# A later weight tile's parts moved behind the second norm's diagonals, and side work held one step earlier

## The chip, the cores and the metric

The kernel runs on one core of a Trainium2 chip. The metric is the device time of one execution in microseconds (us); the median of three runs of the kernel before is 1535.8 us (1535.44 to 1537.49).

## What is computed

One layer of a hybrid decoder block in float32, on 256 rows of width 2048. Cut to what matters here:

```python
mod = SiLU(c) @ ada_w + ada_b            # shift1, scale1, gate1, shift2, scale2, gate2
h   = RMSNorm(x) * (1 + scale1) + shift1
merged = sigmoid(g_A) * (lru(h) @ w_lru_out) + sigmoid(g_B) * (attention(h) @ w_attn_out)
x   = x + gate1 * (merged @ w_o)
h2  = RMSNorm(x) * (1 + scale2) + shift2                     # the second norm
x   = x + gate2 * ((silu(gate) * up) @ w_ffn_out)            # gate, up = h2 @ w_ffn_in
out = RMSNorm(x)
```

## The kernel before

All weights are read once from HBM, in tiles of 128 x 1024 floats (512 KB) that are called items here and numbered in the order of use. Each matmul is done in three products of rounded floats: a weight tile `raw` is split into `hi` (a rounding cast, on ScalarE, `do_hi`, L330) and `lo` (raw minus hi, on VectorE, `do_lo`, L342), an activation likewise, and `mm3` (L380 to L384) multiplies high by high, high by low and low by high. A full item takes 12 matmuls of 512 columns.

The order on every engine is written out by the program. `step(i)` (L349) issues, for item i: the loads up to item i + AHEAD (6) on SyncE's DMA queue, the high parts up to i + N_HI (4) on ScalarE, the low parts up to i + N_LO (3) on VectorE, then the item's matmuls on TensorE, then side work. `raw` has five buffers, `hi` four, `lo` three. Each engine takes its instructions strictly in that order.

Side work here is `ada`: for each of the 96 tiles of 128 values of `mod` (but one) two multiply-and-sum instructions over a 128 x 1024 tile `aw` (L532, VectorE), each with a 512 KB load of its own. `run_sides` places them by a rough clock that the program keeps, wherever that says VectorE has room (`clock["slack"]`); what is not placed in one step comes in a later one. The last of them must be done before the gate of the feed-forward's output is needed.

Around the change stand the last steps of `w_o` (items 268 to 275, the last of its four slabs) and the second norm. `hold_sides` (L1087), put before the last but one step of `w_o`, sets the slack so low that no side work is placed from there on. In the last step the products are sorted so that the first 128 rows' bank is complete half a step before the second's. `second_norm` (L1111) then runs ahead of the next item's step: four transposes for each of x's first four pairs of tiles (`turn`, L1100), and for each half of the rows y = bank * gate1 (L1120), x += y (L1121) and the sum of squares (L1122, ScalarE); two more turns; the root (L1130), its reciprocal, two diagonal blocks, one on VectorE (L1135), one on ScalarE (L1136); two warming matmuls, the product of ones by the diagonals (`r2_ps`, L1139), which lays 1/rms out along the rows, and five more warming matmuls (a float32 matmul shows as two instructions). From `r2_ps` come the normed tiles: `scaled` (L1148, VectorE), `high` (L1156, ScalarE), `low` (L1161, VectorE), pair by pair. Items 276 on are the feed-forward's first weights (`fg`), whose first matmul needs the high part of the first normed tile and whose third needs its low part.

After two slabs of that kind (items 276 to 291) come pairs of slabs in which some blocks are done by seven products for eight; there VectorE also makes sums of weights (`wy`, L458, L459), and `lo` is cut from those sums too.

Of the kernel before, what the change touches and what calls it, by code (L numbers as in the profile page):

```python
# [42 lines left out]
AHEAD, N_HI, N_LO, N_ADA, N_B4 = 6, 4, 3, 2, 25  # L43
# [40 lines left out]
def hybrid_layer(  # L84
# [33 lines left out]
    def wtile(name):  # L118
        return ps.tile([P, 2, S], F32, tag="bank", name=name)
# [8 lines left out]
    def rows(t):  # L128
        return slice(t * P, (t + 1) * P)
# [28 lines left out]
    def keep_warm(n, of_w=False):  # L158

        warm = in_rows_of(wtile("warm")) if of_w else mtile("warm")  # L160
        for _ in range(n):
            nc.tensor.matmul(warm[:, 0:P], lhsT=ones, rhs=ones, start=True, stop=True)
        free(m=0 if of_w else 1)
# [60 lines left out]
    def charge(dve=0.0, act=0.0):  # L224
        clock["dve"] = max(clock["dve"], clock["pe"]) + dve
        clock["act"] = max(clock["act"], clock["pe"]) + act
# [10 lines left out]
    def run_posts():  # L237
        for g in list(posts):
            try:
                charge(*next(g))  # L240
            except StopIteration:
                posts.remove(g)
# [29 lines left out]
    def run_sides(end):  # L272
        for s in sides:
            for _ in range(s.most):
                if s.cost is None:
                    break
                if max(clock["dve"], clock["pe"]) + s.cost[0] > end + clock["slack"]:
                    if s.fits():
                        return
                    break  # L280
                if max(clock["act"], clock["pe"]) + s.cost[1] > end + clock["slack"] or not s.advance():
                    break


    class Item:


        def __init__(self, src, cols, mm, post=None, keep=False, weight=1, used=None, before=()):
# [3 lines left out]

            self.sums = None

    items = []
    live = {}
    at = {"fill": 0, "add": 0, "load": 0, "made": 0, "hi": 0, "lo": 0}

    def do_sum(j):
        def do(i):  # L300
            if items[i].sums is not None:
                items[i].sums[j]()
                load_time(CH)
        return do
# [42 lines left out]
    def upto(what, fn, n):  # L347
        while at[what] < min(n, len(items)):
            fn(at[what])  # L349
            at[what] += 1  # L350

    def step(i):
        it = items[i]
        if not items[min(i + N_LO, len(items)) - 1].keep:
            run_posts()
        upto("load", do_load, i + AHEAD)
        upto("made", do_made, i + N_MADE)
        upto("hi", do_hi, i + N_HI)
        upto("lo", do_lo, i + N_LO)
        if items[min(i + N_LO, len(items)) - 1].keep:  # L360
            run_posts()
        upto("fill", do_sum(0), i + N_SUM[0])
        upto("add", do_sum(1), i + N_SUM[1])
        for stage in it.before:
            charge(*stage())
        for h in streams:
            h.fetch()
        _, hi, lo, t = live.pop(i)
        clock["pe"] = max(clock["pe"], t)
        end = clock["pe"] + it.cols * T_PE * it.weight  # L370
        it.mm(hi, lo)
        run_sides(end)
        clock["pe"] = end
        if it.post is not None:
            posts.append(it.post())
# [686 lines left out]
    def o_post(s):  # L1062
        def post(banks):
            if s == 3:
                second_norm(banks)
                return
            if s == 2:
                early_root()
            y = b4(f"yo{s}", F32, (2, 512))
            for t in range(2):  # L1070
                nc.vector.tensor_tensor(y[:, t, :], in_rows_of(banks[t]), g1_of(s), op=ALU.mult)
            yield 1.4, 0
            nc.vector.tensor_tensor(xr[s], xr[s], y, op=ALU.add)
            yield 1.13, 0
            for t in range(2):
                nc.scalar.activation(y[:, t, :], xr[s][:, t, :], AF.Square, accum_out=ss2[:, t, s:s + 1])
            keep_rows(s)
            free(b4=1)
            yield 0, 1.6
        return post  # L1080
# [8 lines left out]
        clock["slack"] = -1e9  # L1089
        return 0, 0  # L1090

    items[-2].before.append(hold_sides)

    def turn(p, of_w=False):

# [15 lines left out]
    def second_norm(banks):  # L1111
# [22 lines left out]
        r2, diag = b4("r2")[:, 0, :], y[:, 0, 0:S]  # L1134
        nc.vector.tensor_scalar(diag[:, rows(0)], ident, sr[:, 0:1], None, op0=ALU.mult)  # L1135
        nc.scalar.activation(diag[:, rows(1)], ident, AF.Copy, scale=sr[:, 1:2])  # L1136
        r2_ps = wtile("r2_ps")[:, 0, :]
        keep_warm(N_WARM_2[0], True)
        nc.tensor.matmul(r2_ps, lhsT=ones, rhs=diag, start=True, stop=True)  # L1139
# [540 lines left out]
    for i in range(len(items)):  # L1680
        step(i)
# [63 lines left out]
```

## Time and profile before

| | |
|---|---|
| median of three runs | 1535.8 us (1535.44 to 1537.49) |
| the profiled execution | 1538.73 us, its span 1537.0 us |
| granted TensorE clock over the span | 0.998 of full speed |
| TensorE matmuls busy | 1521.0 us, 99% of the span |
| VectorE busy | 1365.3 us, 89% |
| ScalarE busy | 880.7 us, 57% |
| GpSimd busy | 163.5 us, 11% |
| the chain that ended last, by engine | TensorE 93%, DMA 3%, VectorE 3% |

Busy time is the time in which an engine runs instructions, loads of weights into TensorE apart. In the profile PE is TensorE, DVE VectorE, ACT ScalarE, SP SyncE and POOL GpSimd. [...]

### The profile page before, as it was taken

How to read it: one execution, taken by the hardware profiler on the slowest of the kernel's cores; microseconds unless marked ns; L12 is line 12 of the kernel's file. 1: busy time of each engine (PE TensorE's matmuls, PEld its weight loads, DVE VectorE, ACT ScalarE, POOL GpSimd, SP SyncE). 2: the span in 40 equal slices, each digit the busy share in tenths (PEclk: the TensorE clock that was granted, in tenths of full speed). 3: DMA queues.
4: the chain of work that ended last, by engine and by line, in shares of the span. 5: the costliest groups of instructions: out<-in, count | busy, mean ns of one | idle time of the engine just before them, and what ended most of it. 6: DMA issues, size and time to landing. Idle time of an engine off the chain costs nothing.

```text
span 1537.0 us, 20204 instructions
## 1 busy us (share of the span) xinstructions
PE 1521.0 (99%) x6851; PEld 1249.0 (81%) x6851; DVE 1365.3 (89%) x1835; ACT 880.7 (57%) x1142; POOL 163.5 (11%) x232
## 2 busy tenths in 40 slices
PE   8999999999999999999999999999999999999997
PEld 5788888888888787888887878888888888888886
DVE  7999999888898888988988899999999999888987
ACT  4654444886964446444444556656665556664664
POOL 0000000000000000000002231034212122321200
PEclk9999999999999999999999999999999999999999
DMA  9999988656786887999999999589898979989983
GB/s 368 383 345 362 345 315 301 207 181 217 241 286 226 291 308 283 364 325 341 377 373 347 312 338 273 167 254 332 274 273 248 269 243 298 288 257 297 275 266 124
DMA packets 138440, 444.58 MB, mean 289 GB/s; under 512 B 16064, under 2 KB 16224, under 8 KB 138336
## 3 DMA queue, kind: packets, MB, share of 16 engines
q1 hardware_dynamic: 113056, 384.02, 70.2%
q0 software_dynamic: 24992, 58.75, 16.1%
q8 instruction: 53, 0.87, 0.2%
q10 hardware_dynamic: 288, 0.52, 0.1%
q14 instruction: 51, 0.42, 0.1%
HBM read 439.02 MB, written 4.21 MB: 288 GB/s over the span
## 4 chain that ended last, share of the span: by engine, by line
PE 93%; DMA 3%; DVE 3%; ACT 0%; issue 0%; SPq 0%; DVEq 0%; ACTq 0%
PE pf L1391 10%; PE f L383 6%; PE f L382 6%; PE f L384 6%; PE wi L383 6%; PE wi L384 6%; PE wi L382 6%; PE wl L384 2%; PE wl L383 2%; PE wga L384 2%; PE wl L382 2%; PE wga L382 2%; PE wgl L383 2%; PE wga L383 2%; PE wgl L384 2%; PE wa L384 2%
## 5 line engine op out<-in xcount | busy, mean ns | idle before, releaser
L330 ACT CAST hi<-raw 128x1024 fp32r<-128x1024 f32 (+1 forms) x540 | 532.3, 996 | 419.1 <-PE wi L384 87.4
L342 DVE TENSOR_TENSOR lo<-raw,hi 128x1024 fp32r<-128x1024 f32 (+1 forms) x540 | 611.9, 1149 | 82.1 <-issue 37.7
L383 PE MATMUL wi<-lo,h 128*128 128x512 f32 x432 | 168.4, 390 | 3.3 <-DVE lo L342 3.3
L382 PE MATMUL wi<-hi,h 128*128 128x512 f32 x432 | 169.9, 393 | 0.0
L384 PE MATMUL wi<-hi,h 128*128 128x512 f32 x432 | 168.2, 389 | 0.0
L382 PE MATMUL f<-hi,h 128*128 128x512 f32 x406 | 158.8, 391 | 0.0
L383 PE MATMUL f<-lo,h 128*128 128x512 f32 x406 | 158.1, 389 | 0.0
L384 PE MATMUL f<-hi,h 128*128 128x512 f32 x406 | 158.0, 389 | 0.0
L532 DVE CUSTOM_DVE_ANT_0 aw<-aw,crow,vec 128x1024 f32<-128x1024 f32 x95 | 120.5, 1277 | 6.0 <-DMA aw<-in_ada_t_dram 6.0
L532 DVE CUSTOM_DVE_ANT_0 aw<-aw,crow,modc 128x1024 f32<-128x1024 f32 x95 | 121.1, 1277 | 1.6 <-DMA aw<-in_ada_t_dram 1.6
L330 ACT CAST hi<-wy 128x1024 fp32r<-128x1024 f32 x55 | 58.0, 1055 | 74.3 <-PE f L384 32.1
L383 PEld LDWEIGHTS wi<-lo,h 128*128 128x128 f32 x432 | 81.1, 188 | 20.9 <-DVE lo L342 4.3
L342 DVE TENSOR_TENSOR lo<-wx,hi 128x1024 fp32r<-128x1024 f32 x55 | 67.2, 1222 | 32.4 <-issue 28.5
L330 ACT CAST hi<-wx 128x1024 fp32r<-128x1024 f32 x55 | 58.0, 1055 | 64.8 <-PE pf L1391 24.0
L382 PEld LDWEIGHTS wi<-hi,h 128*128 128x128 f32 x432 | 81.1, 188 | 16.8 <-ACT acc L611 0.2
L384 PEld LDWEIGHTS wi<-hi,h 128*128 128x128 f32 x432 | 81.1, 188 | 16.7
L384 PEld LDWEIGHTS f<-hi,h 128*128 128x128 f32 x406 | 76.2, 188 | 15.8
L383 PEld LDWEIGHTS f<-lo,h 128*128 128x128 f32 x406 | 76.2, 188 | 15.7 <-DVE lo L342 0.3
L382 PEld LDWEIGHTS f<-hi,h 128*128 128x128 f32 x406 | 76.2, 188 | 15.6
L447 POOL DMA_DIRECT2D wx<-in_w_f_dram x78 | 69.8, 969 | 79.5 <-DMA wx<-in_w_f_dram 78.4
L443 POOL DMA_DIRECT2D wx<-in_w_f_dram x78 | 44.7, 627 | 287.6 <-DVE lo L342 95.2
L342 DVE TENSOR_TENSOR lo<-wy,hi 128x1024 fp32r<-128x1024 f32 x55 | 67.2, 1222 | 6.9 <-ACT hi L330 4.3
(347 smaller groups left out, 3094.1 us busy)
## 6 DMA issues: line engine op xcount, KB each, us to landing
aw<-in_ada_t_dram SPq DMA_DIRECT2D x190, 512.0 KB, 6.7
raw<-in_w_in_dram SPq DMA_DIRECT2D x164, 512.0 KB, 5.1
raw<-in_w_f_dram SPq DMA_DIRECT2D x137, 512.0 KB, 6.5
wx<-in_w_f_dram POOLq DMA_DIRECT2D x156, 256.0 KB, 7.9
raw<-in_w_f2a_dram SPq DMA_DIRECT2D x36, 512.0 KB, 6.4
raw<-in_w_lru_dram SPq DMA_DIRECT2D x32, 512.0 KB, 4.6
raw<-in_w_att_dram SPq DMA_DIRECT2D x32, 512.0 KB, 5.5
raw<-in_w_o_dram SPq DMA_DIRECT2D x32, 512.0 KB, 8.1
```

What stands on the lines that cost most here:

```text
L330: nc.scalar.copy(hi[:, cs], live[i][0][:, cs])
L342: nc.vector.tensor_tensor(lo[:, cs], raw[:, cs], f32(hi[:, cs]), op=ALU.subtract)
L382: nc.tensor.matmul(ps, lhsT=lh, rhs=rh, start=start, stop=False, skip_group_check=True)
L383: nc.tensor.matmul(ps, lhsT=lh, rhs=rl, start=False, stop=False, skip_group_check=True)
L384: nc.tensor.matmul(ps, lhsT=ll, rhs=rh, start=False, stop=stop, skip_group_check=True)
L443: nc.gpsimd.dma_start(x[:, j * 512:(j + 1) * 512], block(0, 1))
L447: nc.gpsimd.dma_start(got["x"][:, j * 512:(j + 1) * 512], block(j, j), accum_op=ALU.add)
L532: nc.vector.tensor_tensor_reduce(out=r, in0=r, in1=crow[j], op0=ALU.mult, op1=ALU.add, scale=1.0, scalar=dst if j else vec[:, v:v + 1], ac ...
L1391: nc.tensor.matmul(bank(t, n), lhsT=l[:, rows(t)], rhs=w[:, c0:c0 + 512], start=kt == 0 and k == 0, stop=kt == (EARLY - 2 if (t, n) == (1, ...
```

## The change

Side work is held from the last step but two of `w_o` on, not the last but one. In the last step of `w_o` the high and the low parts go one item less far ahead (`parts_wait`), and the two parts that are left out there, the high part of item 278 and the low part of item 277, are issued inside `second_norm` right behind the two diagonal blocks. Nothing is added or removed.

```diff
@@ -292,6 +292,8 @@
             self.sums = None
+            self.parts_wait = 0
...
@@ -355,8 +357,9 @@
         upto("load", do_load, i + AHEAD)
         upto("made", do_made, i + N_MADE)
-        upto("hi", do_hi, i + N_HI)
-        upto("lo", do_lo, i + N_LO)
+
+        upto("hi", do_hi, i + N_HI - it.parts_wait)
+        upto("lo", do_lo, i + N_LO - it.parts_wait)
...
@@ -1089,7 +1092,8 @@
         clock["slack"] = -1e9
         return 0, 0
-    items[-2].before.append(hold_sides)
+    items[-3].before.append(hold_sides)
+    items[-1].parts_wait = 1
...
@@ -1134,6 +1138,9 @@
         nc.vector.tensor_scalar(diag[:, rows(0)], ident, sr[:, 0:1], None, op0=ALU.mult)
         nc.scalar.activation(diag[:, rows(1)], ident, AF.Copy, scale=sr[:, 1:2])
+
+        upto("hi", do_hi, at["hi"] + 1)
+        upto("lo", do_lo, at["lo"] + 1)
         r2_ps = wtile("r2_ps")[:, 0, :]
```

TensorE's and GpSimd's order is the same in both. The lines of the changed kernel are higher by 2 to 7 (L342 is L344 there, L532 is L535, L1120 is L1124, L1148 is L1155).

VectorE from the last two steps of `w_o` to the first normed tile (`lo275` is the last item of `w_o`, `aw` with its line L532 is side work, shown as two instructions). Before:

```order
L342 TENSOR_TENSOR lo275_6925<-raw275_6858,hi275_6902 128x1024
L532 ISA aw179_6886,modc_162<-aw179_6886,crow0_108,vec_74 128x1024
L532 ISA modc_162 128x1
L342 TENSOR_TENSOR lo276_6946<-raw276_6880,hi276_6923 128x1024
L342 TENSOR_TENSOR lo277_6964<-raw277_6900,hi277_6944 128x1024
L1120 TENSOR_TENSOR yo3_7008<-wo3_0_0_6821,g11_6095 128x512
L1121 TENSOR_TENSOR xr3_6819<-xr3_6819,yo3_7008 128x512
L1120 TENSOR_TENSOR yo3_7008<-wo3_0_1_6822,g11_6095 128x512
L1121 TENSOR_TENSOR xr3_6819<-xr3_6819,yo3_7008 128x512
L1106 COPY x1T1_7024<-pt1_6993 128x512
L1129 TENSOR_REDUCE sr_7023<-ss2_176 128x2
```

And now, up to the first normed tile:

```order
L344 TENSOR_TENSOR lo275_6925<-raw275_6858,hi275_6902 128x1024
L344 TENSOR_TENSOR lo276_6945<-raw276_6880,hi276_6923 128x1024
L1124 TENSOR_TENSOR yo3_7003<-wo3_0_0_6821,g11_6095 128x512
L1125 TENSOR_TENSOR xr3_6819<-xr3_6819,yo3_7003 128x512
L1124 TENSOR_TENSOR yo3_7003<-wo3_0_1_6822,g11_6095 128x512
L1125 TENSOR_TENSOR xr3_6819<-xr3_6819,yo3_7003 128x512
L1110 COPY x1T1_7019<-pt1_6988 128x512
L1133 TENSOR_REDUCE sr_7018<-ss2_176 128x2
L1135 RECIPROCAL sr_7018<-sr_7018 128x2
L1139 TENSOR_SCALAR yo3_7003<-ident_92,sr_7018 128x128
L344 TENSOR_TENSOR lo277_7039<-raw277_6900,hi277_6943 128x1024
L1155 SCALAR_TENSOR_TENSOR x1T0_7007<-x1T0_7007,modc_162,r2_ps_7041 128x256 x2
```

Two instructions are gone from in front of the norm's first one, the multiply `aw179` and `lo277`; `lo277` now stands between the diagonal block and the first `scaled`.

ScalarE at the same place, now (before, the cast `hi278` stood right behind `hi277`):

```order
L332 CAST hi277_6943<-raw277_6900 128x1024
L1126 ACTIVATE yo3_7003,ss2_176<-xr3_6819 128x512
L1110 COPY x1T0_7007<-pt0_6983 128x512
L1126 ACTIVATE yo3_7003,ss2_176<-xr3_6819 128x512
L1134 ACTIVATE sr_7018<-sr_7018,eps_t_90 128x2
L1140 ACTIVATE yo3_7003<-ident_92,sr_7018 128x128
L332 CAST hi278_7037<-raw278_6921 128x1024
L1163 ACTIVATE h2_0_6975<-x1T0_7007,modc_162 128x256 x2
```

The cast moved from ahead of the squares to ahead of the first `high`.

The multiply that is not done before the norm pushes the ones behind it on. Eleven now stand behind the norm where ten stood. The last of them are in the first pair of slabs on VectorE. Before:

```order
L342 TENSOR_TENSOR lo304_7664<-raw304_7625,hi304_7651 128x1024
L532 ISA aw189_7558,modc_162<-aw189_7558,crow1_109,modc_162 128x1024
L532 ISA modc_162 128x1
L458 TENSOR_TENSOR wy_7681<-wx_7432,raw305_7635 128x512
L459 TENSOR_TENSOR wy_7681<-wy_7681,raw304_7625 128x512
L342 TENSOR_TENSOR lo305_7686<-raw305_7635,hi305_7662 128x512
L342 TENSOR_TENSOR lo306_7704<-wx_7432,hi306_7684 128x1024
```

Now:

```order
L344 TENSOR_TENSOR lo304_7663<-raw304_7624,hi304_7650 128x1024
L535 ISA aw188_7530,modc_162<-aw188_7530,crow1_109,modc_162 128x1024
L535 ISA modc_162 128x1
L461 TENSOR_TENSOR wy_7680<-wx_7430,raw305_7634 128x512
L462 TENSOR_TENSOR wy_7680<-wy_7680,raw304_7624 128x512
L344 TENSOR_TENSOR lo305_7685<-raw305_7634,hi305_7661 128x512
L535 ISA aw189_7602,modc_162<-aw189_7602,crow1_109,modc_162 128x1024
L535 ISA modc_162 128x1
L344 TENSOR_TENSOR lo306_7704<-wx_7430,hi306_7683 128x1024
```

Between `lo304` and `lo306` there are two multiplies where there was one. On SyncE's queue three of the loads of `aw` (185, 187 and 189) have moved behind one weight load each.

## Rows read from the trace of the kernel before

**Rows 1.** The page: busy time of TensorE (share of the span, instructions), and the chain that ended last, by engine.

```profile
PE 1521.0 (99%) x6851; PEld 1249.0 (81%) x6851; DVE 1365.3 (89%) x1835; ACT 880.7 (57%) x1142; POOL 163.5 (11%) x232
PE 93%; DMA 3%; DVE 3%; ACT 0%; issue 0%; SPq 0%; DVEq 0%; ACTq 0%
```

**Rows 2.** What TensorE waited for over the whole span: engine, tile and line that waited, who ended the wait, us in total, times, longest.

```profile
PE pt L1100 <- DVE xr L1121: 1.0, 1, 1.0
PE r_ps L1139 <- ACT yo L1136: 0.9, 1, 0.9
```

**Rows 3.** Timeline of VectorE around the second norm and, last, in the slab behind it: start us, us, engine, line, operation, out<-in, shapes, count, and in brackets the idle time before and what ended it.

```profile
820.63 1.28 DVE L532 CUSTOM_DVE_ANT_0 aw<-aw,crow,vec 128x1024 f32<-128x1024 f32 x1 [2.02 <-DMA aw<-in_ada_t_dram]
821.84 1.22 DVE L342 TENSOR_TENSOR lo<-raw,hi 128x1024 fp32r<-128x1024 f32 x1
823.40 1.23 DVE L342 TENSOR_TENSOR lo<-raw,hi 128x1024 fp32r<-128x1024 f32 x1 [0.34 <-ACT hi L330]
824.54 0.68 DVE L1120 TENSOR_TENSOR yo<-wo,g 128x512 f32<-128x512 f32 x1
...
825.87 0.68 DVE L1120 TENSOR_TENSOR yo<-wo,g 128x512 f32<-128x512 f32 x1
...
828.80 0.29 DVE L1135 TENSOR_SCALAR yo<-ident,sr 128x128 f32<-128x128 f32 x1
830.12 0.87 DVE L1148 SCALAR_TENSOR_TENSOR x1T<-x1T,modc,r_ps 128x256 f32<-128x256 f32 x2 [1.03 <-PE r_ps L1139]
831.23 0.89 DVE L1161 SCALAR_TENSOR_TENSOR h<-x1T,modc,h 128x256 fp32r<-128x256 f32 x2 [0.24 <-ACT h L1156]
...
834.68 1.21 DVE L342 TENSOR_TENSOR lo<-raw,hi 128x1024 fp32r<-128x1024 f32 x1
...
854.82 1.23 DVE L342 TENSOR_TENSOR lo<-raw,hi 128x1024 fp32r<-128x1024 f32 x1 [1.50 <-PE fg L383]
```

**Rows 4.** Timeline of ScalarE there, same columns.

```profile
822.32 1.05 ACT L330 CAST hi<-raw 128x1024 fp32r<-128x1024 f32 x1 [3.54 <-DMA raw<-in_w_f_dram]
824.88 1.05 ACT L330 CAST hi<-raw 128x1024 fp32r<-128x1024 f32 x1 [1.51 <-DMA raw<-in_w_f_dram]
...
828.80 0.40 ACT L1136 ACTIVATE yo<-ident,sr 128x128 f32<-128x128 f32 x1 [0.23 <-DVE sr L1131]
830.69 0.91 ACT L1156 ACTIVATE h<-x1T,modc 128x256 fp32r<-128x256 f32 x2 [1.49 <-DVE x1T L1148]
```

**Rows 5.** Timeline of TensorE there, same columns (ends of matmuls are modelled, so a matmul's us reach past the start of the next).

```profile
821.69 0.39 PE L384 MATMUL wo<-hi,ml 128*128 128x512 f32 x1
...
823.05 0.39 PE L384 MATMUL wo<-hi,ml 128*128 128x512 f32 x1
823.28 3.06 PE L1100 MATMUL pt<-ident,xr 128*128 128x128 f32 x25
827.34 0.55 PE L1100 MATMUL pt<-ident,xr 128*128 128x128 f32 x3 [1.00 <-DVE xr L1121]
827.72 0.61 PE L162 MATMUL warm<-ones 128*128 128x128 f32 x4
829.25 0.83 PE L1139 MATMUL r_ps<-yo,ones 128*128 128x256 f32 x2 [0.92 <-ACT yo L1136]
829.87 2.34 PE L162 MATMUL warm<-ones 128*128 128x128 f32 x10
831.86 0.77 PE L382 MATMUL fg<-hi,h 128*128 128x512 f32 x1
...
835.29 0.60 PE L1100 MATMUL pt<-ident,xr 128*128 128x128 f32 x4
835.64 0.48 PE L382 MATMUL fg<-hi,h 128*128 128x512 f32 x1
...
838.47 0.39 PE L382 MATMUL fg<-hi,h 128*128 128x512 f32 x1
```

**Rows 6.** Stretches of the span: from:to us, length, busy us (and instructions) of PE, PEld, DVE, ACT and POOL, granted TensorE clock, DMA share, GB/s. The second is from the start of the kernel.

```profile
829.00:834.00 5.00, 4.75 (x19) 4.27 (x20) 3.54 (x10) 2.27 (x6) 2.85 (x4) 0.66 1.04 401
18.00:20.00 2.00, 0.92 (x8) 0.72 (x7) 1.71 (x4) 0.23 (x2) 0.00 (x0) 1.00 1.04 414
```

**Rows 7.** Timeline of TensorE at the first norm, where the same product of ones by diagonals (rx_ps) and ten warming instructions ran at the full clock.

```profile
17.00 0.60 PE L1630 MATMUL rx_ps<-sqx,ones 128*128 128x256 f32 x2
17.44 1.28 PE L162 MATMUL warm<-ones 128*128 128x128 f32 x10
```

**Rows 8.** Timeline of ScalarE, VectorE and TensorE in the first pair of slabs: high and low part of item 304, the multiply `aw189`, the low part of item 306 and the first matmul on the low part of item 310.

```profile
900.00 1.05 ACT L330 CAST hi<-raw 128x1024 fp32r<-128x1024 f32 x1 [1.60 <-DMA raw<-in_w_f_dram]
901.09 1.23 DVE L342 TENSOR_TENSOR lo<-raw,hi 128x1024 fp32r<-128x1024 f32 x1 [0.87 <-ACT hi L330]
902.23 1.28 DVE L532 CUSTOM_DVE_ANT_0 aw<-aw,crow,modc 128x1024 f32<-128x1024 f32 x1
...
905.37 1.22 DVE L342 TENSOR_TENSOR lo<-wx,hi 128x1024 fp32r<-128x1024 f32 x1
...
911.98 0.50 PE L383 MATMUL fr<-lo,hs 128*128 128x512 f32 x1 [0.17 <-DVE lo L342]
```

**Rows 9.** Stretches of the span, columns as in rows 6.

```profile
848.00:852.00 4.00, 4.00 (x19) 3.34 (x18) 3.37 (x5) 2.76 (x4) 1.12 (x2) 1.00 0.67 222
890.00:900.00 10.00, 9.93 (x44) 7.71 (x43) 9.93 (x15) 4.74 (x6) 3.07 (x5) 1.00 1.08 305
```

## The prediction

> **What bounds the kernel now.** I began with the page's busy times and its chain: TensorE is busy for 99% of the span and makes up 93% of the chain [rows 1]. So the end comes earlier only if TensorE waits less, works less or runs at a better clock, and anything on another engine counts only where TensorE waits for it. The view of TensorE's waits comes next, since it names those places: of what is left, the second norm has the two waits of rows 2, 1.0 us for x's last rows from VectorE and 0.9 us for the diagonal from ScalarE [rows 2]. Both lie in the stretch that the change edits, so the rest is read from the timelines of the three engines there.
>
> On TensorE the last matmul of w_o starts at 823.05, and the first of the feed-forward at 831.86 [rows 5]. Between them lies a chain that begins on VectorE. Its first instruction (yo, L1120) starts at 824.54 [rows 3], although the bank that it reads was complete when the matmul of 821.69, 0.39 long, ended: 822.08 [rows 5]. It is late because VectorE takes its instructions in order: a multiply at 820.63, which had waited 2.02 us for its load, then two low parts, the second of which waited for its high part until 823.40 [rows 3]. That high part waited for its load until 822.32 [rows 4]. From there it is one after another: sums, root, diagonals at 828.80, the product at 829.25, normed tiles from 830.12 [rows 3 to 5].
>
> The stretches add a second cost: from 829 to 834 the granted clock was 0.66 in the mean [rows 6]. [...]
>
> **The change, part by part.**
>
> *Ahead of the norm.* The multiply of 820.63 is gone, and with it the wait for its load; the low part at 821.84 moves up to where its input is ready, and the one at 823.40 leaves [rows 3]. VectorE is then free before the bank is complete, so yo starts at 822.1 instead of 824.54. Its second half needs the second bank, complete at 823.05 + 0.39 = 823.44 [rows 5], so it starts at 823.47 instead of 825.87: 2.4 us earlier [rows 3]. What follows it up to the diagonals depends on that alone: they start at 828.80 - 2.4 = 826.4, ScalarE's ends at 826.8 [rows 3, 4].
>
> *The product.* TensorE has its own queue ahead of it: 28 transposes at 3.06/25 = 0.12 us from 823.28, then four warming instructions of 0.13 us (1.28/10) [rows 5, 7]. It gets there at 823.28 + 3.4 + 0.5 = 827.15, after the diagonals. So the product starts 2.1 us earlier, TensorE stays without a gap, and this is the new limit. At the full clock product and drain took 0.60 us [rows 7]: ready at 827.75.
>
> *The low part behind the diagonal.* On VectorE it starts when the diagonal block has been made, 826.4 + 0.3, and holds the engine for 1.14 us (823.40 to the next start at 824.54) [rows 3]: until 827.8. Queued behind it is the first normed tile, for which everything waits. What hides it is TensorE's queue and product, which last until 827.75; nearly all is covered, and without that cover it would cost up to 1.14. The normed tiles start at 827.8 instead of 830.12: 2.3 us earlier [rows 3].
>
> *The high part behind the diagonal.* On ScalarE 826.8 to 827.9; behind it is the first high, which can't start before 827.8 + 0.57 (830.12 to 830.69) [rows 3, 4]. It costs nothing as long as its tile has landed, as it had by 824.88 [rows 4].
>
> *TensorE into the feed-forward.* Ten warming instructions start 0.44 after the product and take 1.28 [rows 7]: until 828.9. The first high is ready at 827.8 + 0.57 + 0.46 = 828.8, the first low, needed two matmuls later, at 827.8 + 1.11 + 0.44 = 829.35 [rows 3, 4]. So the first matmul moves from 831.86 to 828.9. At the full clock its item takes 12 matmuls at a pitch of 0.23 us (823.05 to 823.28), and four transposes 0.35 (835.29 to 835.64): the next item starts at 828.9 + 2.75 + 0.35 = 832.0 instead of 835.64 [rows 5]. **3.7 us**, of which 0.7 is clock in that one item. [...] The lower end is 2.1, the product's own shift, if the clock falls as before; 3.9 is the upper one, for what the modelled ends leave open. Nothing behind takes it back at once: the low part due for the item at 838.47 was done at 834.68 + 1.21 [rows 3, 5]. VectorE's chain is 2.3 us earlier and TensorE 3.7, so the margin of 2.6 shrinks to 1.2.
>
> *The multiply that was pushed on.* It is done later, at 1.20 us (902.23 to 903.43, the next start; its row has 1.28) [rows 8]. In the two slabs behind the norm VectorE waits for TensorE, as at 854.82 for 1.50 us [rows 3], and swallows it. In the first pair of slabs it doesn't: the order there has two multiplies between the low parts of items 304 and 306 where one stood. Before, the low part of 304 started at 901.09 when a load had at last let its high part begin at 900.00, VectorE ran from there without a pause, and TensorE waited for the low part of item 310 until 911.98 [rows 8]. Thus 1.2 us more between 304 and 310 is 1.2 us later on TensorE: **+1.2**. The ends are 0 (item 304 comes early enough) and +1.28. The three loads of aw that move behind a weight load each I cost at nothing: their multiplies move later too, and 512 KB at the 305 GB/s of that stretch is 1.7 us against that [rows 9].
>
> **Sum.** -3.7 + 1.2 = -2.5 us. The profiled execution took 1538.73 us with a span of 1537.0: that becomes 1536.2 and 1534.5. The median of the runs is 2.9 us below the profiled execution; taken from it, 1535.8 - 2.5 = **1533.3 us**. About 0.2%, 3.1 us, is what a measurement of this kernel can tell from no change, so the forecast is a small gain that may not be seen as one. With each term's ends near the likely value its own range is 1532.5 to 1534.2.
>
> **Rivals.**
>
> *The pushed multiply is covered too.* If the load of item 304 comes early enough, VectorE is ahead there, and 3.7 us remain: 1532.1. For it: between the low parts of items 297 and 300 the new order has one multiply fewer, so VectorE reaches 304 with time to spare. Against it: what 304 waited for was a load [rows 8].
>
> *The clock falls all the same.* Then the way from the product to the second item takes what it took, 835.64 - 829.25 [rows 5], and only 2.1 us come from the norm; with +1.2, 0.9 us: 1534.9. Against it: a single spell of 1.1 us without work left the clock at 1.00 (0.92 us busy of two, from 18 to 20) [rows 6], and after the change some 0.1 to 0.4 us are left. For it: what let it fall was not one gap, and the transposes and warming work are all that fills the stretch. [...]
>
> *The transfers don't move, and the end is slower.* If the load of item 304 lands at the same 900.0 though TensorE and VectorE come 3.7 us earlier, item 304 starts at 901.09 as before and the second multiply sets TensorE back: +1.2, 1537.0. It decides when that landing moves by less than 1.2 us. For it: the DMA share was 1.08 from 890 to 900 and the cast waited 1.60 us for its tile [rows 8, 9]. Against it: from 848 to 852 the share was 0.67 [rows 9], so no backlog reaches across, and the loads behind it are issued when VectorE frees a buffer, thus earlier.
>
> *The norm does not move.* Something else than VectorE's order holds yo, or a tile lands late in front of the diagonals' followers (ScalarE's cast waits for one, then the first high waits for the cast). Then the time stays near 1535.8 or somewhat above.
>
> **How the numbers follow.** Forecast 0.50, covered multiply 0.20, clock 0.14, transfers 0.08, norm unmoved 0.08. Faster by over 0.2% means below 1532.7: most of the covered case and a fifth of the forecast's, 0.28. Slower by over 0.2% means above 1538.9, which no case reaches but by a late tile: 0.03. The rest, 0.69, is within. The range takes in the forecast, the covered multiply and the clock, and leaves out the last two cases; with 0.5 us for the scatter of a median it is 1531.6 to 1535.4.
>
> **What would show it.** Right: yo starts about 822.1, second half 823.5, the product about 827.2, TensorE with no wait in rows 2's places, clock 1.00 throughout, the feed-forward's first matmul about 828.9, and between items 304 and 310 a wait of TensorE longer by 1 us than before. Wrong: yo or the product where they were; a stretch at 0.50; a wait on the first normed tile behind the moved low part; no wait near item 306, which gives the covered case.

## The result: 0.16% slower, and the profile after

The changed kernel took 1539.03 us in the median of 18 runs (1536.74 to 1540.89), the kernel before 1536.18 us (18 runs beside them, 1535.14 to 1537.75): a ratio of 1.0016 (of the means; of the medians it is 1.0019), 95% interval 1.001 to 1.0023. The median is 2.85 us higher where 2.5 lower had been forecast, and above the range, which ended at 1535.4. Its profiled execution has a span of 1538.5 us and took 1540.32.

At the norm the profile after looks as the prediction said. VectorE there (start us, us, engine, line, operation, out<-in, shapes, count, idle time before in brackets), against [rows 3]:

```profile
821.77 0.69 DVE L1124 TENSOR_TENSOR yo<-wo,g 128x512 f32<-128x512 f32 x1 [3.01 <-PE wo L387]
...
823.13 0.69 DVE L1124 TENSOR_TENSOR yo<-wo,g 128x512 f32<-128x512 f32 x1
...
826.06 0.29 DVE L1139 TENSOR_SCALAR yo<-ident,sr 128x128 f32<-128x128 f32 x1
826.26 1.22 DVE L344 TENSOR_TENSOR lo<-raw,hi 128x1024 fp32r<-128x1024 f32 x1
827.40 0.86 DVE L1155 SCALAR_TENSOR_TENSOR x1T<-x1T,modc,r_ps 128x256 f32<-128x256 f32 x2
```

The first half of yo starts at 821.77 and now waits for TensorE, which is as it should be; the low part stands behind the diagonal block, and the first normed tile follows without a wait. TensorE, against [rows 5]:

```profile
822.93 3.22 PE L1104 MATMUL pt<-ident,xr 128*128 128x128 f32 x28
...
826.52 0.70 PE L1146 MATMUL r_ps<-yo,ones 128*128 128x256 f32 x2
827.05 1.28 PE L162 MATMUL warm<-ones 128*128 128x128 f32 x10
828.53 0.50 PE L385 MATMUL fg<-hi,h 128*128 128x512 f32 x1 [0.20 <-ACT h L1163]
...
831.80 0.48 PE L385 MATMUL fg<-hi,h 128*128 128x512 f32 x1
```

The second item of the feed-forward starts at 831.80 instead of 835.64, 3.84 us earlier (the forecast's term was 3.7; 0.35 of it was there before the norm, since the transposes start at 822.93 instead of 823.28), the warming work runs at its full-clock 1.28, and from 829 to 834 the clock is 1.00 where it was 0.66 [rows 6]. Up to 894 every item keeps those 3.8 us. They are lost in the first pair of slabs. TensorE there:

```profile
894.93 0.39 PE L386 MATMUL f<-lo,h 128*128 128x512 f32 x1
...
897.72 0.51 PE L385 MATMUL f<-hi,h 128*128 128x512 f32 x1
898.98 0.50 PE L386 MATMUL f<-lo,h 128*128 128x512 f32 x1 [0.76 <-DVE lo L344]
...
902.98 0.39 PE L385 MATMUL f<-hi,hs 128*128 128x512 f32 x1
904.59 0.50 PE L386 MATMUL f<-lo,hs 128*128 128x512 f32 x1 [1.22 <-DVE lo L344]
...
905.16 0.40 PE L385 MATMUL fr<-hi,hs 128*128 128x512 f32 x1
906.93 0.50 PE L386 MATMUL fr<-lo,hs 128*128 128x512 f32 x1 [1.38 <-DVE lo L344]
907.27 0.47 PE L387 MATMUL fr<-hi,hs 128*128 128x512 f32 x1
...
910.92 0.39 PE L387 MATMUL f<-hi,h 128*128 128x512 f32 x1
...
911.39 0.40 PE L386 MATMUL fp<-lo,h 128*128 128x512 f32 x1
```

894.93 is the first low-part matmul of item 302, 911.39 that of item 308: 16.46 us, where the first trace of before had 10.36. In them TensorE waits three times for a low part (lo) and then runs slowly. Matmuls follow each other at 0.23 us otherwise; 897.72 to 898.98, 902.98 to 904.59 and 905.16 to 906.93 are 4.64, thus 3.95 too long, and the nine steps from 907.27 to 910.92 took 3.65 instead of 2.1. The stretches (from:to, length, busy us and counts of PE, PEld, DVE, ACT, POOL, granted clock, DMA share, GB/s) show the latter as clock:

```profile
890.00:900.00 10.00, 9.12 (x39) 7.00 (x38) 5.64 (x7) 4.48 (x5) 2.81 (x5) 1.00 1.07 337
900.00:907.00 7.00, 4.40 (x19) 2.99 (x17) 6.79 (x10) 4.23 (x6) 3.87 (x6) 1.00 1.08 260
907.00:911.00 4.00, 4.00 (x11) 3.14 (x12) 3.96 (x5) 1.04 (x1) 1.07 (x2) 0.57 1.05 379
```

0.57 in the last: a stretch at 0.50 (0.50 in each half microsecond from 907.5 to 910.5), as the trace of before had at the norm (0.50 from 830 to 833), now stands behind the three waits. VectorE and ScalarE in the same place, against [rows 8]:

```profile
897.70 1.23 DVE L344 TENSOR_TENSOR lo<-raw,hi 128x1024 fp32r<-128x1024 f32 x1 [3.24 <-ACT hi L332]
900.17 1.23 DVE L344 TENSOR_TENSOR lo<-raw,hi 128x1024 fp32r<-128x1024 f32 x1 [1.25 <-ACT hi L332]
901.32 1.28 DVE L535 CUSTOM_DVE_ANT_0 aw<-aw,crow,modc 128x1024 f32<-128x1024 f32 x1
...
903.85 0.68 DVE L344 TENSOR_TENSOR lo<-raw,hi 128x512 fp32r<-128x512 f32 x1
904.45 1.28 DVE L535 CUSTOM_DVE_ANT_0 aw<-aw,crow,modc 128x1024 f32<-128x1024 f32 x1
...
905.66 1.22 DVE L344 TENSOR_TENSOR lo<-wx,hi 128x1024 fp32r<-128x1024 f32 x1
```

```profile
896.62 1.05 ACT L332 CAST hi<-raw 128x1024 fp32r<-128x1024 f32 x1 [3.90 <-DMA raw<-in_w_f_dram]
899.09 1.05 ACT L332 CAST hi<-raw 128x1024 fp32r<-128x1024 f32 x1 [1.43 <-DMA raw<-in_w_f_dram]
```

The high parts of items 303 and 304 wait for their loads until 896.62 and 899.09, only 0.9 us earlier than before for the latter (900.00 [rows 8]) though everything ahead of it had come 3.8 us earlier. Behind them stand two modulation multiplies (901.32, 904.45) where one stood. From the pair on nothing more is lost: from item 308 to the end both traces take the same time within 0.3 us (619.3 and 619.6).

### The profile page after: what moved, and what is told of

Its sections match the earlier page's. It is cut to its first block, busy times and chain, and to the rows that moved or that the text cites. A ratio compares the mean times of both kernels' runs of the same rounds, so it can differ in the third digit from the quotient of the medians.

```text
span 1538.5 us, 20202 instructions
## 1 busy us (share of the span) xinstructions
PE 1521.1 (99%) x6851; PEld 1249.0 (81%) x6851; DVE 1365.2 (89%) x1835; ACT 880.3 (57%) x1142; POOL 163.5 (11%) x232
## 4 chain that ended last, share of the span: by engine, by line
PE 92%; DMA 4%; DVE 2%; ACT 0%; issue 0%; SPq 0%; DVEq 0%; ACTq 0%
PE pf L1398 10%; PE f L385 6%; PE f L386 6%; PE f L387 6%; PE wi L387 6%; PE wi L386 6%; PE wi L385 6%; PE wl L387 2%; PE wgl L386 2%; PE wl L386 2%; PE wga L387 2%; PE wl L385 2%; PE wga L385 2%; PE wga L386 2%; PE wa L387 2%; PE wgl L387 2%
## 5 line engine op out<-in xcount | busy, mean ns | idle before, releaser
L344 DVE TENSOR_TENSOR lo<-raw,hi 128x1024 fp32r<-128x1024 f32 (+1 forms) x540 | 612.2, 1150 | 85.3 <-issue 40.7
L535 DVE CUSTOM_DVE_ANT_0 aw<-aw,crow,vec 128x1024 f32<-128x1024 f32 x95 | 120.6, 1278 | 3.0 <-DMA aw<-in_ada_t_dram 3.0
L535 DVE CUSTOM_DVE_ANT_0 aw<-aw,crow,modc 128x1024 f32<-128x1024 f32 x95 | 121.2, 1279 | 0.9 <-DMA aw<-in_ada_t_dram 0.9
L344 DVE TENSOR_TENSOR lo<-wx,hi 128x1024 fp32r<-128x1024 f32 x55 | 67.2, 1223 | 30.5 <-issue 27.1
L344 DVE TENSOR_TENSOR lo<-wy,hi 128x1024 fp32r<-128x1024 f32 x55 | 67.2, 1223 | 7.7 <-ACT hi L332 4.5
```

Of the source, the lines that this page charges most:

```text
L344: nc.vector.tensor_tensor(lo[:, cs], raw[:, cs], f32(hi[:, cs]), op=ALU.subtract)
L535: nc.vector.tensor_tensor_reduce(out=r, in0=r, in1=crow[j], op0=ALU.mult, op1=ALU.add, scale=1.0, scalar=dst if j else vec[:, v:v + 1], ac ...
```

## Experiments

The theories, as the expectations name them. A: the loads of 303 and 304 set that place. B: VectorE's queue does, with the pushed multiply in it. C: the clock falls there for a cause of its own. D, formed when the first four were in: the kernel before loses time at the norm in some executions only, so most have nothing to give. Its rival is E (every execution has it). F: the loads' lateness alone loses, whichever multiplies stand behind them.

All kernels in one table. "Norm" is the time on TensorE from the start of the transposes behind w_o (L1100 before) to the first matmul of the feed-forward, "pair" that from the first low-part matmul of item 302 to that of item 308, both from the kernel's trace.

| kernel | median us (runs) | before beside it | ratio, 95% | norm | pair |
|---|---|---|---|---|---|
| before, first trace | | | | 8.58 | 10.36 |
| before_again | 1535.97 (1) | 1536.35 | | 5.59 | 10.37 |
| after | 1539.03 (18) | 1536.18 | 1.0016 (1.001 to 1.0023) | 5.60 | 16.46 |
| after_again | 1543.69 (1) | 1536.35 | | 5.59 | 16.79 |
| hold_only | 1539.22 (11) | 1535.65 | 1.0019 (1.001 to 1.0027) | 5.76 | 14.77 |
| parts_only | 1536.42 (11) | 1535.65 | 1.0001 (0.9992 to 1.001) | 5.59 | 11.77 |
| loads_out | 1535.5 (11) | 1535.65 | 0.9996 (0.9988 to 1.0005) | 5.59 | 10.20 |
| mults_out | 1536.46 (11) | 1535.65 | 1.0003 (0.9995 to 1.0012) | 5.59 | 10.86 |
| late_a | 1535.73 (11) | 1536.35 | 0.9997 (0.9988 to 1.0006) | 5.60 | 10.20 |
| late_one | 1535.2 (11) | 1536.11 | 0.9994 (0.9985 to 1.0003) | 5.60 | 10.20 |
| late_one_again | 1535.29 (11) | 1536.37 | 0.9997 (0.9988 to 1.0006) | 5.60 | 10.20 |
| late_b | 1535.89 (11) | 1536.11 | 0.9998 (0.9989 to 1.0007) | 5.46 | 10.20 |
| load_late_before | 1542.61 (4) | 1536.11 | 1.0044 (1.0029 to 1.0059) | 11.52 | 10.43 |
| load_late_after | 1538.74 (10) | 1536.11 | 1.0015 (1.0005 to 1.0024) | 5.59 | 13.24 |

**hold_only and parts_only: the two halves of the change.**

```diff
 hold_only (of the changed kernel)
...
-    items[-1].parts_wait = 1
...
-        upto("hi", do_hi, at["hi"] + 1)
-        upto("lo", do_lo, at["lo"] + 1)
 parts_only (of the changed kernel)
...
-    items[-3].before.append(hold_sides)
+    items[-2].before.append(hold_sides)
```

> The change without its moved parts: side work is held from the last step but two of w_o, and the weight parts stand where they stood before. Theory A (the landing of the loads of items 303 and 304 sets that place, so what is gained ahead of it beyond about 0.9 us is lost there, and the pushed multiply and a stretch at clock 0.50 are added): the norm gives 1 to 2 us, the loads of 303 and 304 land less than 1 us earlier, items 305 to 308 lose as in the changed kernel, end 0 to 2 us above before. Theory B (only VectorE's queue with the pushed multiply costs): norm 1 to 2 us earlier less 1.2, end -0.8 to +0.2 us.

> The change without its earlier hold: the parts of the later weight tile stand behind the diagonals, and the side multiply stays where it was before. Theory A (landing of 303 and 304): the norm gives 1 to 2 us, no multiply is pushed, items 303 and 304 start about 0.9 us earlier than before, end -1.0 to 0 us. Theory B (only the pushed multiply costs): all of the norm's gain is kept, end -1 to -2 us. In both no stretch at clock 0.50 between 900 and 912.

The loss comes with the hold: hold_only is as slow as the whole change (+3.6 us), its pair takes 14.77. The moved parts alone cost 1.4 us in the pair in their trace, which is of the longest of their 11 executions (1538.06), and nothing that the runs can tell (+0.8 us, ratio 1.0001). Both ends lie above what either theory allowed (at most +2 and 0). What neither expected is the norm: each half alone has 5.76 or 5.59 there, as good as both, against 8.58 in the trace of before. Where either half alone seems to bring the whole gain, the gain may belong to neither: the trace of before was in doubt.

**loads_out and mults_out: the loads or the multiplies taken away.**

```diff
 loads_out (of the changed kernel; taken counts the multiplies)
...
-                nc.sync.dma_start(t, self.srcs[self.n])
+                if self.n < 186:
+                    nc.sync.dma_start(t, self.srcs[self.n])
...
-                        out=r, in0=r, in1=crow[j],
+                        out=r, in0=r if halves.taken <= 186 else crow[j], in1=crow[j],
 mults_out (of the changed kernel; taken as above)
...
+                    w = CH if halves.taken <= 188 else 8
...
-                        out=r, in0=r, in1=crow[j],
+                        out=r[:, :w], in0=r[:, :w], in1=crow[j][:, :w],
```

> The changed kernel with the loads of the last four modulation tiles (2 MB, issued at 869 to 878) left out; their four multiplies stay in place at full size, on resident rows, so four of the modulation sums are not those of the reference. Theory A (transfers): the loads of 303 and 304 land 3 us or more earlier than in the changed kernel, TensorE keeps 3.8 us through item 304, the waits of 305 and 306 on the low parts shrink to under 0.5 us, no stretch at 0.50 there, end 2.5 to 3.5 us below before. Theory B (VectorE's queue): multiplies still stand ahead of the low parts of 305 and 306, waits of over 1 us stay, end within 0.7 us of the changed kernel's +2.8.

> The changed kernel with the last two modulation multiplies (901 and 904) cut to 8 columns, their loads kept, so two modulation sums are not those of the reference. Theory A (transfers): items 303 and 304 still start only about 3 us earlier than before, since the loads land as in the changed kernel (waits of 0.8 us stay at 303), but 305 to 308 then lose little: end 1.5 to 3 us below before. Theory B (VectorE's queue): all waits on low parts go, 3.8 us kept, end 3.5 us below before. Theory C (the stretch at clock 0.50 comes for another cause than the waits): it stays, and the end is no lower than 1.5 us below before.

Either cure is enough: the pair falls to 10.20 and 10.86. In loads_out both multiplies are there, and no wait on a low part in the pair; in mults_out the loads were late, though 1.9 us less than in the changed kernel's trace, and TensorE waited 0.33 us. VectorE and ScalarE in mults_out:

```profile
898.95 1.23 DVE L344 TENSOR_TENSOR lo<-raw,hi 128x1024 fp32r<-128x1024 f32 x1 [1.40 <-ACT hi L332]
900.10 0.22 DVE L537 CUSTOM_DVE_ANT_0 aw<-aw,crow,modc 128x8 f32<-128x8 f32 x1
...
902.17 0.22 DVE L537 CUSTOM_DVE_ANT_0 aw<-aw,crow,modc 128x8 f32<-128x8 f32 x1
...
902.32 1.22 DVE L344 TENSOR_TENSOR lo<-wx,hi 128x1024 fp32r<-128x1024 f32 x1
```

```profile
895.24 1.05 ACT L332 CAST hi<-raw 128x1024 fp32r<-128x1024 f32 x1 [1.86 <-DMA raw<-in_w_f_dram]
897.87 1.05 ACT L332 CAST hi<-raw 128x1024 fp32r<-128x1024 f32 x1 [1.58 <-DMA raw<-in_w_f_dram]
```

How late the loads are can be told from the start of item 304's high part against the first low-part matmul of item 302, and set beside the multiplies that stand between the low parts of 304 and 306 (load_late_after is described below):

| trace | 304's high part behind item 302, us | multiplies | pair, us |
|---|---|---|---|
| loads_out | -1.37 | 2 | 10.20 |
| before_again | 0.35 | 1 | 10.37 |
| mults_out | 2.28 | 2 of 8 columns | 10.86 |
| parts_only | 2.28 | 1 | 11.77 |
| load_late_after | 2.51 | 2 | 13.24 |
| hold_only | 2.61 | 2 | 14.77, with a stretch at 0.50 |
| after | 4.16 | 2 | 16.46, with a stretch at 0.50 |

So A and B are each half right: two multiplies behind timely loads cost nothing, loads that are 2.3 to 2.6 us late cost 0.7 us without a full multiply, 1.6 with one and 3.0 with two (4.6 where the clock fell too), against the 10.20 of the undisturbed pair. Loads as late as the changed kernel's 4.16 were not tried without the multiplies. C falls: where the waits go (none on a low part in the pair of loads_out, 0.5 us in all there and behind it in mults_out), the stretch at 0.50 goes (1.00 from 890 to 917 in both). In both traces TensorE is 3 us and more earlier than in the first trace of before, but the medians are not: 1535.5 and 1536.46 beside 1535.65, where A had ends of 1.5 to 3.5 us below before. The missing 3 us had to lie in before.

**before_again and after_again: each kernel a second time, unchanged.**

> The kernel before, unchanged, a second trace. The first was of an execution of 1538.73, 2.9 above the median. Theory D (the stretch at clock 0.50 at the second norm, 829 to 833, is in some executions only, and the forecast priced it as if it were in all): this one takes 1535 to 1536, its clock is 1.00 at the norm, TensorE's first item behind the norm starts 1.5 to 3 us nearer to the last item of w_o than the 17.9 us of the first trace, and the change's own gain at the norm is what is left, 0.5 to 2 us. Theory E (the norm is the same in every execution): that distance is the same within 0.3 us, and the difference to the first trace lies elsewhere.

> The changed kernel, unchanged, a second trace. If the loss in the first pair of slabs (items 303 to 308) comes from order and transfers, it is here again: 3.5 to 6 us lost between items 302 and 309, 1.7 more with a stretch at clock 0.50 than without. If it came from one execution's chance, it is under 1 us.

Theory D. VectorE, then TensorE, at the norm of before_again:

```profile
817.68 1.28 DVE L532 CUSTOM_DVE_ANT_0 aw<-aw,crow,vec 128x1024 f32<-128x1024 f32 x1 [0.39 <-DMA aw<-in_ada_t_dram]
818.89 1.22 DVE L342 TENSOR_TENSOR lo<-raw,hi 128x1024 fp32r<-128x1024 f32 x1
821.50 1.22 DVE L342 TENSOR_TENSOR lo<-raw,hi 128x1024 fp32r<-128x1024 f32 x1 [1.40 <-PE wo L383]
823.03 0.69 DVE L1120 TENSOR_TENSOR yo<-wo,g 128x512 f32<-128x512 f32 x1 [0.31 <-PE wo L384]
```

```profile
824.20 3.22 PE L1100 MATMUL pt<-ident,xr 128*128 128x128 f32 x28
...
827.91 0.70 PE L1139 MATMUL r_ps<-yo,ones 128*128 128x256 f32 x2
...
829.79 0.50 PE L382 MATMUL fg<-hi,h 128*128 128x512 f32 x1
```

The multiply ahead of yo waited 0.39 us for its load, not 2.02 [rows 3]; the second low part was done before yo could start, and yo waited for TensorE. The 28 transposes run through, the product follows, and the first feed-forward matmul comes 5.59 us behind the first transpose: what the changed kernel has, so that nothing is left of the gain where D still expected 0.5 to 2 us. This execution took 1535.97, close to the medians; the first trace was of one of 1538.73. And the loss of the changed kernel is there again in after_again, 16.79, 6.4 us against the 3.5 to 6 expected. (The 1543.69 of that execution lies above all 18 runs of the changed kernel; 2.9 us of it were there before the norm, whose transposes start at 825.85 against 822.93 in the first trace.) In before_again the pair goes as follows, ScalarE, then VectorE:

```profile
894.37 1.05 ACT L330 CAST hi<-raw 128x1024 fp32r<-128x1024 f32 x1 [0.24 <-DMA raw<-in_w_f_dram]
896.94 1.05 ACT L330 CAST hi<-raw 128x1024 fp32r<-128x1024 f32 x1 [1.52 <-DMA raw<-in_w_f_dram]
```

```profile
898.03 1.22 DVE L342 TENSOR_TENSOR lo<-raw,hi 128x1024 fp32r<-128x1024 f32 x1 [0.36 <-ACT hi L330]
899.17 1.28 DVE L532 CUSTOM_DVE_ANT_0 aw<-aw,crow,modc 128x1024 f32<-128x1024 f32 x1
...
902.31 1.22 DVE L342 TENSOR_TENSOR lo<-wx,hi 128x1024 fp32r<-128x1024 f32 x1
```

TensorE reached item 302 at 896.59: the high part of 303 began 2.2 us before that, in the changed kernel 1.7 us after it (896.62 against 894.93), and one multiply follows instead of two.

**late_a, late_one, late_b: the last modulation tiles held over the place.** Four tiles (loads and multiplies) in late_a and late_b, the last one in late_one; late_b is the kernel before with this edit. late_one_again is late_one a second time. The loads are let go 20 items into the first pair of slabs.

```diff
 late_one (late_a and late_b: 186)
         sides[:] = [ada]
+        halves.limit = 189
...
+        if s == SLAB_7:
+            items[start + 20].before.append(fetch_on)
...
+    def fetch_on():
+        halves.limit = len(halves.srcs)
+        return 0, 0
```

> The changed kernel with the last four modulation tiles (their loads and multiplies) held until the later part of the first pair of slabs (about 925), where the DMA share falls to 0.5; everything is computed. Theory A (transfers) and theory B (VectorE's queue): both take the four loads and two multiplies out of the place, so the low parts of 304 to 306 are in time, the 3.5 us behind the norm are kept through item 309. Against the median of before: theory D 1534 to 1535.7 (the norm's gain is small in most executions), theory E 1532 to 1533. A multiply among VectorE's 18.1 us busy of 20 in 940 to 1000 could hold TensorE there by up to 1 us.

> The changed kernel with only the last modulation tile (one load, one multiply: the one that the earlier hold pushes on) held until the later part of the first pair of slabs; everything is computed. Theory A (the pushed multiply is what loses: it comes behind low parts that a late load has delayed already): items 302 to 309 lose 0 to 1.5 us instead of 6, end within 0.7 us of before. Theory F (the loss is the loads' own lateness, whichever multiplies stand there): still 2.5 us or more lost, end 1538 to 1539.

> The kernel before with the last four modulation tiles held until the later part of the first pair of slabs, as in late_a; everything is computed. Theory D (in most executions the change gives nothing at the norm): same time as late_a, 1535.7, within 0.5 us, both 0 to 0.7 us below before. Theory E (the change gives 2 us or more there in every execution): 2 us above late_a.

> The changed kernel with the last modulation tile held, a second time. If it is better than before in most executions: again 0.5 to 1 us below, the interval of the ratio below 1 or touching it. If the 0.9 us of the first time were chance: within 0.3 us of before. Its second trace again loses under 1 us between items 302 and 309.

late_one undoes just the push, by holding one multiply and its load. Its place in VectorE's timeline:

```profile
893.99 3.49 DVE L344 TENSOR_TENSOR lo<-raw,hi 128x1024 fp32r<-128x1024 f32 x3
897.40 1.28 DVE L535 CUSTOM_DVE_ANT_0 aw<-aw,crow,modc 128x1024 f32<-128x1024 f32 x1
...
901.08 1.23 DVE L344 TENSOR_TENSOR lo<-wx,hi 128x1024 fp32r<-128x1024 f32 x1 [0.46 <-issue]
```

Three low parts one after another (their high parts had been made in one run from 892.57 on, without a wait for a load, that of 304 from about 894.5; in before_again that one waited for its load until 896.94), one multiply, and VectorE is ahead again; the pair takes 10.20. That is A's number and not F's. But the loads came earlier too, so what the multiplies do behind late loads is shown by mults_out and the table above, not here. late_a and late_b come out 0.16 us apart (0.62 and 0.22 below the befores beside them), although only the first has the change: D, and against E, which had 2 us between them. late_one has the lowest medians of all, 0.9 and 1.1 us below before, but both intervals take in 1. It is the best version found and not shown to be faster. (In late_a the held loads are issued from 912 on. The DMA share of the changed kernel there was 1.03 from 915 to 925 and 0.87 from 925 to 935, not the 0.5 that the expectation names; 0.52 comes from 960 to 980.)

**load_late_before and load_late_after: the load of the norm's multiply issued later.**

```diff
 both
-                nc.sync.dma_start(t, self.srcs[self.n])
+                if self.n != 179:
+                    nc.sync.dma_start(t, self.srcs[self.n])
+                if self.n == 181:
+                    nc.sync.dma_start(self.put_off, self.srcs[179])
+                if self.n == 179:
+                    self.put_off = t
```

> The kernel before with one load moved: that of the modulation tile whose multiply stands ahead of the norm's first instruction is issued behind two more weight loads and two modulation loads (812.7 instead of 808.7). Theory D (what the change saves at the norm is the wait of that multiply for its load, 2.02 us in the first trace and 0.39 in the second): the multiply waits 3 us or more, the norm's first instruction starts 2 to 4 us later than in the second trace of before, end 2 to 5 us above before, with or without a stretch at 0.50. Rival: VectorE makes it up before TensorE needs it, end within 1 us of before.

> The changed kernel with the same load moved. The multiply stands behind the norm here. Theory D: the norm takes what it took in the changed kernel (first feed-forward item 5.6 us behind the start of the last transposes), end as the changed kernel, 2 to 3.5 us above before, so that the two kernels come out equal within 2 us although one is 2.8 slower without the moved load. Rival: the moved load costs here too, 2 us above the changed kernel.

VectorE at the norm of load_late_before, then of load_late_after:

```profile
824.11 1.28 DVE L537 CUSTOM_DVE_ANT_0 aw<-aw,crow,vec 128x1024 f32<-128x1024 f32 x1 [7.25 <-DMA aw<-in_ada_t_dram]
...
825.32 2.35 DVE L342 TENSOR_TENSOR lo<-raw,hi 128x1024 fp32r<-128x1024 f32 x2
827.59 0.68 DVE L1125 TENSOR_TENSOR yo<-wo,g 128x512 f32<-128x512 f32 x1
```

```profile
822.76 0.69 DVE L1129 TENSOR_TENSOR yo<-wo,g 128x512 f32<-128x512 f32 x1 [3.02 <-PE wo L387]
```

The multiply waits 7.25 us for its load, yo starts at 827.59, TensorE waits for x's rows (2.50 and 1.00 us), the stretch at 0.50 comes (0.75 in the mean from 824 to 836), and the kernel is 6.5 us slower, more than the 2 to 5 expected. The changed kernel with the same load takes 5.59 at the norm and is no slower than without it (1538.74 and 1539.03). So the mechanism that the prediction described is real. It pays where that load is late, and there the changed kernel is 3.9 us the faster one.

One more thing shows beside hold_only. TensorE in the pair of hold_only, then of load_late_after:

```profile
903.96 0.50 PE L386 MATMUL f<-lo,hs 128*128 128x512 f32 x1 [1.15 <-DVE lo L344]
...
906.30 0.80 PE L386 MATMUL fr<-lo,hs 128*128 128x512 f32 x1 [1.38 <-DVE lo L344]
```

```profile
903.95 0.50 PE L386 MATMUL f<-lo,hs 128*128 128x512 f32 x1 [1.04 <-DVE lo L344]
...
906.29 0.50 PE L386 MATMUL fr<-lo,hs 128*128 128x512 f32 x1 [1.38 <-DVE lo L344]
```

The waits differ by 0.11 us, but the clock fell in the first (0.57 in the mean from 906 to 910) and stayed at 1.00 in the second; the pairs are 14.77 and 13.24.

## Why the prediction was wrong

- **Ahead of the norm, the product, the parts behind the diagonals, TensorE into the feed-forward (-3.7).** Each step came as told: yo 821.77 (forecast 822.1), second half 823.13 (823.5), first normed tile 827.40 (827.8), first feed-forward matmul 828.53 (828.9); 3.84 us. But the term was taken off the median, and the median execution, as far as the runs show, has nothing to take off: the norm took 8.58 in one trace of before, 5.59 in the other, 5.59 or 5.60 in the changed kernel, and late_a and late_b, with and without the change, end 0.16 us apart. **This is the step that failed**: "The median of the runs is 2.9 us below the profiled execution; taken from it, 1535.8 - 2.5". Those 2.9 us and the 3.0 at the norm are about the same, and they begin with the wait of 2.02 us for a load [rows 3]. Counted from the second trace the term is 0.
- **The multiply that was pushed on (+1.2).** Its place, between the low parts of 304 and 306, was right, its size wrong: 6.1 us in the pair (16.46 - 10.37), 6.4 in the second trace. Both traces are of executions above the median (1540.32 and 1543.69 against 1539.03), so these sizes are no more typical than the first trace of before was. Traces of hold_only and load_late_after, whose executions lay at their medians, have 4.4 and 2.9 us, nearer to the 2.85 of the medians. The term was priced as VectorE's own 1.2 us with the loads where they were. The loads came later against TensorE (3.9 us for the high part of 303), the low parts of 303 to 306 with them, and in both traces the clock's fall behind the waits added about 1.6.
- **The three loads of aw, costed at nothing.** Not shown to be innocent: with the last one held, the loads of 302 to 304 land earlier (in late_one no high part of them waits for its load, in the changed kernel those of 303 and 304 wait until 896.62 and 899.09) and the loss is gone (10.20 us in the pair).
- **Clock 1.00 throughout.** Wrong in both traces of the changed kernel: 0.57 from 907 to 911 in one, 0.81 from 912 to 917 in the other, always behind the waits in the pair. One kernel can have the fall in one execution and not in another: from 829 to 834 the clock was 0.66 in the one trace of before [rows 6], 1.00 in the other. These two traces don't tell why, since TensorE's waits differ too: 1.00 and 0.92 us in the one [rows 5], none in the other. hold_only and load_late_after come nearer, with waits 0.11 us apart and a fall in one only (0.57 from 906 to 910 against 1.00 from 900 to 917); what decided there, no run shows.
- **The rivals.** "The transfers don't move, and the end is slower" is what happened, by its own mark: the cast of item 304 began 0.9 us earlier than in rows 8, under its 1.2 (and 2.2 us later than in before_again). It was given a chance of 0.08, since the share of 0.67 from 848 to 852 [rows 9] was read as an end of the backlog; from 870 on the share was 1.05 to 1.07 in the changed kernel, and that is the stretch in which these loads were issued. Its time, 1537.0, counted the norm's gain as lost on the way, and is 2.0 us short because it had the pushed multiply at 1.2. "The norm does not move" is what the second trace of before gives (5.59 against 5.60), but not for the reasons named: in that execution nothing held the norm up.

Still open: why the loads of 303 and 304 land later in the changed order. In mults_out, which is the changed kernel up to 900, the high part of 303 started 0.35 us before item 302 (895.24, 895.59), in the changed kernel 1.69 after it; part of it is scatter between executions. How often an execution of before has the late load at the norm was not counted either; two traces show one with and one without. Of the 108 timed executions of before beside the runs four took over 1538 us and none the 1538.73 of the first trace.

## What to carry to other kernels

Before a wait is priced, see whether the profiled execution is a typical one: where it lies above the median by as much as the gain that it promises, take a second trace first. Work that is pushed out of one tight place has to be followed to where it lands, and priced there with the loads late, not as it stood in one trace. Where a late load and a full queue each have some margin, hold back either; here moving one side tile (512 KB and 1.28 us) behind the tight place took the whole loss away (10.20 us in the pair, against 16.46).

## What the runs showed of the hardware

- Two executions of one unchanged program (before, before_again) differed by 3.0 us in one stretch of 9 (8.58 and 5.59 us at the norm), by a load that landed late (VectorE's multiply waited 2.02 us for it in the one, 0.39 in the other) and the stretch at clock 0.50 that followed (0.66 in the mean from 829 to 834, against 1.00).
- At the norm and in the pair the stretch at 0.50 came in or behind the last of several waits, not of one idle spell: 1.00 and 0.92 us in the first trace of before (0.50 from 830 to 833), 0.76, 1.22 and 1.38 us with matmuls between them in the changed kernel (0.57 in the mean from 907 to 911), 1.15 and 1.38 in hold_only (0.57 from 906 to 910), 2.50 and 1.00 in load_late_before (0.75 in the mean from 824 to 836). In load_late_after, waits of 1.04, 1.38 and, 5.3 us later, 0.17 us left the clock at 1.00 (from 900 to 917).
- With a DMA share of 1.05 to 1.07 from 870 to 900 in the changed kernel, holding one load of 512 KB back (late_one) went with the next ones landing earlier: the high part of item 304 began at about 894.5 in late_one, without a wait for its load, at 899.09 in the changed kernel, behind 1.43 us of waiting for it, and at 897.87 in mults_out, which has the same loads, behind 1.58. That is at least 4.6 and 3.4 us, more than the 1.6 us that its bytes take at 330 GB/s (an estimate from the rate in late_one from 890 to 900); the 1.2 us between the last two are scatter, and how much of the rest is scatter was not measured.
